# Feed-forward up projection from seven block products, and a down projection that reads its activations back from DRAM

## The chip, the cores and the metric

One core of a Trainium2 chip runs the whole program. The metric is the device time of one execution in microseconds (us). The kernel before was timed in three runs: median 1926.27 us, from 1924.97 to 1929.52. A matmul here has a weight of 128 x 128 and a moving operand of 128 x 512 or 128 x 256; float32 operands are split into a high and a low part (`hi`, `lo`), and a product takes three matmuls (hi·hi, hi·lo, lo·hi).

## The reference, cut to what matters

One decoder layer over 1024 tokens of width 1024. The change touches its last part only:

```
x = x + merged @ w_out
u = rmsnorm(x) * norm_ffn
h = causal_dwconv3(u @ w_up)          # w_up: 1024 x 5632, three taps along the tokens, plus a bias
g, val = split(h, 2)                  # 2816 = 22 tiles of 128 channels each
x = x + (silu(g) * val) @ w_down      # w_down: 2816 x 1024
out = rmsnorm(x) * norm_final
```

## The kernel before, in words

All data lie with channels on the 128 partitions and tokens along the columns. `x2` (L833) holds x as eight tiles j of 128 channels x 1024 tokens. `out_tile(j, h, w)` (L843) adds merged @ w_out for tile j and token half h, and adds the squares to `ss`. `rms_rows` (L170) turns `ss` into 1/RMS along the columns of a PSUM bank; it has two small parts on TensorE, four transposes each. `norm2(h)` (L857) then scales each of the eight tiles of half h on VectorE (DVE), casts the high part on ScalarE (ACT), and subtracts for the low part on VectorE or GpSimd (POOL), tile by tile (`scale_split`, L189).

The up projection has 44 column tiles, gate and value tile of one f tile in turn. `up(i)` (L884) loads one tile of weights (512 KB, `load_w`, L103: DMA, cast on ACT, subtraction on DVE), and for each token half runs 8 contraction tiles x 3 matmuls of 512 columns into one bank. The convolution is taken straight from that bank: one activation on ACT and two multiply-adds on DVE per half. The first halves of three column tiles run while the second half of the tokens is normalised (L912). `act_group` (L920) makes the activations of two f tiles, split, and keeps them in SBUF. The down projection follows two f tiles later: `down` (L935) takes 6 matmuls for an output tile and a token half, and adds the bank to `x2` on DVE. The last four f tiles are taken by tokens (512, 256, 256; L981), and each set of tokens is normalised and stored beside the next.

Every engine and the DMA queue of SyncE (SP) runs its instructions in order. What that order is, is fixed when the program is built: a planner (`schedule_with_timeline_sim`, L1078) takes, engine by engine, the earliest instruction of the program text whose inputs are there by its own estimate of time. `step` (L184) pins TensorE work behind a given instruction. Buffers come from pools with tags; a tile of the same tag waits until the last reader of the one before it is done. PSUM has seven working banks in this part (L831). The small tiles `sq` and `ut` share four buffers of tag `tmp`.

## Time and profile before

| what | value |
|---|---|
| median of three runs | 1926.27 us (1924.97 to 1929.52) |
| profiled execution | span 1923.5 us; the page gives it by its span alone |
| busy share of the span | TensorE 98%, VectorE 54%, ScalarE 39%, GpSimd 8% |
| mean granted TensorE clock | 0.995 of full speed |
| instructions on TensorE | 8916 matmuls |

The span is the time from the first to the last instruction of one profiled execution. A busy share is an average over stages with different limits; a stage has to be read by itself. The part that the change rewrites runs from 1183.67 us, the first matmul of the up projection, to the end of the span.

### The profile page before, as it was taken

The page shows a single profiled execution, that of the slowest core. Times are in us where ns is not written, and L with a number is a line of the kernel's source. Part 1 is how long each engine was busy: PE and PEld are TensorE (multiplying, and loading weights), DVE is VectorE, ACT ScalarE, POOL GpSimd, SP SyncE. Part 2 cuts the span into 40 slices and gives each one's busy share as a digit, 9 for nine tenths or more (in the row PEclk, how much of TensorE's full clock was granted, in tenths as well). Part 3 has the DMA queues.
Part 4 walks back from the last instruction along what each step waited for, and adds up shares of the span by engine and source line. Part 5 has one row for each costly group of instructions (what it writes and reads, how often), then busy time and mean ns, then how long its engine had stood idle before and what let it go on. Part 6 is the DMA issues. An engine that isn't in the chain of part 4 may idle for free.

```text
span 1923.5 us, 22457 instructions
## 1 busy us (share of the span) xinstructions
PE 1891.8 (98%) x8916; PEld 1555.9 (81%) x8916; DVE 1033.5 (54%) x1697; ACT 748.8 (39%) x1210; POOL 144.9 (8%) x122
## 2 busy tenths in 40 slices
PE   7999999999999999999999999999999999999997
PEld 6888888888878787877888887888888888888887
DVE  5742782751365554656664426654555455545546
ACT  5353682662355554546432313422222222222232
POOL 0100330420000000000040022000000000000002
PEclk9999999999999999999999999999999999999999
DMA  4230231433412223125453410111111111111112
GB/s 149 95 104 33 99 111 34 135 116 110 167 42 86 79 82 102 41 99 181 164 176 112 150 55 34 55 44 52 47 44 55 44 55 44 44 55 44 55 44 88
DMA packets 60235, 160.20 MB, mean 83 GB/s; under 512 B 6561, under 2 KB 13153, under 8 KB 59618
## 3 DMA queue, kind: packets, MB, share of 16 engines
q1 hardware_dynamic: 57392, 149.38, 22.5%
q0 software_dynamic: 1728, 8.39, 1.3%
q8 instruction: 70, 1.15, 0.2%
q10 hardware_dynamic: 1010, 1.00, 0.2%
q14 instruction: 35, 0.29, 0.0%
HBM read 127.71 MB, written 31.03 MB: 83 GB/s over the span
## 4 chain that ended last, share of the span: by engine, by line
PE 94%; DVE 2%; ACT 2%; DMA 1%; issue 1%; POOL 0%; SPq 0%; ACTq 0%; DVEq 0%; POOLq 0%
PE p_bank L119 42%; PE p_big L119 19%; PE p_half L119 16%; PE p_bank L261 2%; PE p_bank L260 2%; PE p_bank L259 2%; PE p_po L718 2%; PE p_sc L670 2%; PE p_pt L693 2%; PE p_sc L669 1%; PE p_bank L553 1%; PE p_bank L320 0%; DMA yps<-yp_d 0%; PE p_bank L807 0%; ACT mt L518 0%
## 5 line engine op out<-in xcount | busy, mean ns | idle before, releaser
L101 DVE TENSOR_TENSOR wlo<-wraw,whi 128x1024 fp32r<-128x1024 f32 x146 | 183.9, 1260 | 319.2 <-ACT whi L108 319.1
L108 ACT CAST whi<-wraw 128x1024 fp32r<-128x1024 f32 x146 | 153.3, 1050 | 438.2 <-PE p_bank L119 316.5
L119 PE MATMUL p_bank<-u2h,whi 128*128 128x512 f32 x704 | 274.7, 390 | 0.0
L119 PE MATMUL p_bank<-u2l,whi 128*128 128x512 f32 x704 | 274.6, 390 | 0.0
L119 PE MATMUL p_bank<-u2h,wlo 128*128 128x512 f32 x704 | 274.4, 390 | 0.0
L119 PE MATMUL p_bank<-act,whi 128*128 128x512 f32 (+1 forms) x720 | 210.9, 376 | 0.0
L899 DVE SCALAR_TENSOR_TENSOR ffn_tmp<-p_bank,vec,ffn_tmp 128x511 f32<-128x511 f32 (+1 forms) x176 | 131.3, 746 | 95.0 <-ACT ffn_tmp L897 93.5
L119 PE MATMUL p_big<-uh,whi 128*128 128x512 f32 (+1 forms) x416 | 157.6, 379 | 0.5 <-ACT whi L108 0.5
L119 PE MATMUL p_big<-uh,wlo 128*128 128x512 f32 (+1 forms) x416 | 157.5, 379 | 0.5 <-DVE wlo L101 0.5
L119 PE MATMUL p_big<-ul,whi 128*128 128x512 f32 (+1 forms) x416 | 157.0, 378 | 0.0
L119 PEld LDWEIGHTS p_bank<-u2h,wlo 128*128 128x128 f32 x704 | 132.5, 188 | 27.6
L119 PEld LDWEIGHTS p_bank<-u2l,whi 128*128 128x128 f32 x704 | 132.5, 188 | 27.5
L119 PEld LDWEIGHTS p_bank<-u2h,whi 128*128 128x128 f32 x704 | 132.5, 188 | 27.5
L119 PE MATMUL p_half<-uh,whi 128*128 128x512 f32 x384 | 153.5, 400 | 0.0
L119 PE MATMUL p_half<-ul,whi 128*128 128x512 f32 x384 | 153.2, 399 | 0.0
L119 PE MATMUL p_half<-uh,wlo 128*128 128x512 f32 x384 | 152.4, 397 | 0.0
L119 PEld LDWEIGHTS p_bank<-act,whi 128*128 128x128 f32 x720 | 132.2, 188 | 24.5
L944 DVE TENSOR_TENSOR x<-x,p_bank 128x512 f32<-128x512 f32 (+1 forms) x168 | 109.2, 659 | 52.8 <-PE p_bank L119 52.2
L119 PE MATMUL p_bank<-act,wlo 128*128 128x512 f32 (+1 forms) x360 | 135.4, 376 | 0.0
L168 POOL TENSOR_TENSOR ss<-ss,sq 128x512 f32<-128x512 f32 (+1 forms) x24 | 29.0, 1210 | 841.3 <-ACT sq L167 841.1
L897 ACT ACTIVATE ffn_tmp<-p_bank,vec 128x512 f32<-128x512 f32 x88 | 68.2, 775 | 58.7 <-PE p_bank L119 58.6
L119 PEld LDWEIGHTS p_big<-uh,wlo 128*128 128x128 f32 x416 | 79.1, 190 | 14.6 <-DVE wlo L101 0.8
(267 smaller groups left out, 3353.3 us busy)
## 6 DMA issues: line engine op xcount, KB each, us to landing
wraw<-in_w_in_dram SPq DMA_DIRECT2D x48, 512.0 KB, 3.3
wraw<-in_f_up_dram SPq DMA_DIRECT2D x44, 512.0 KB, 3.2
g_d<-gt SPq DMA_DIRECT2D x48, 256.0 KB, 2.0
gt<-g_d SPq DMA_DIRECT2D x48, 256.0 KB, 3.4
wraw<-in_f_down_dram SPq DMA_DIRECT2D x22, 512.0 KB, 3.2
mt<-acs_d SPq DMA_DIRECT2D x16, 512.0 KB, 4.1
xt<-in_x_dram SPq DMA_DIRECT2D x8, 512.0 KB, 7.5
wraw<-in_w_z_dram SPq DMA_DIRECT2D x8, 512.0 KB, 3.2
```

The costliest lines, as they stand in the source:

```text
L101: eng.tensor_tensor(lo, src, hi.bitcast(F32), op=ALU.subtract)
L108: nc.scalar.copy(hi, raw)
L119: m = nc.tensor.matmul(o, lhsT=wt, rhs=ah[part], start=first and i == 0, stop=last and i == 2)
L259: nc.tensor.matmul(ps, lhsT=a, rhs=hi[:, c], start=k == 0, stop=False)
L260: nc.tensor.matmul(ps, lhsT=a, rhs=lo[:, c], start=False, stop=False)
L261: nc.tensor.matmul(ps, lhsT=ul[t // 4][:, k, q], rhs=hi[:, c], start=False, stop=k == NT - 1)
L670: nc.tensor.matmul(pss[:, 0:w], lhsT=Q2[h][hp, qs], rhs=KL[hp, j0:j0 + w], start=False, stop=True)
L693: nc.tensor.transpose(pt[:, off + (i - qq[0]) * P:off + (i - qq[0] + 1) * P], in_=probs[i][:, kb * P:(kb + 1) * P], identity=ident)
L718: nc.tensor.matmul(po[:, q0:q0 + w], lhsT=VV[:, kb, h, :], rhs=t[:, o:o + w], start=pc == 0 and i == 0, stop=last and i == len(prods) - 1)
L897: nc.scalar.activation(a, ps, AF.Identity, bias=vec[:, V_FB + i:V_FB + i + 1], scale=w[2])
L899: nc.vector.scalar_tensor_tensor(out=a[:, s:], in0=ps[:, 0:512 - s], scalar=w[2 - s], in1=a[:, s:], op0=ALU.mult, op1=ALU.add)
L944: nc.vector.tensor_tensor(o, o, ps, op=ALU.add)
```

## The change

The up projection of one f tile is a product of 2 x 2 blocks: the weights of its gate tile (A11 and A12, contraction tiles 0 to 3 and 4 to 7) and of its value tile (A21, A22), times the normalised tokens (B11 and B21 for tokens 0 to 511, B12 and B22 for 512 to 1023). The change forms it from seven block products of 12 matmuls, with sums of blocks as operands. The sums of the weights, S1 to S4, are made for every f tile on GpSimd (`up_sums`). The sums of the tokens, T1 to T4, are made once, in `norm_second`. The seven weight blocks of an f tile are split into a ring of ten buffers, ten products ahead (`split_next`); six of them exist until the second normalisation is through. The products land in four banks (`pair`; `first_pair` for the first f tile, in another order), and VectorE and ScalarE add them up in one tile `cc` (`ca` gate, `cb` value, 1024 tokens each). `conv_act` convolves from `cc` and writes the activations to DRAM (`act_d`).

The down projection comes afterwards, in four passes: token half h, output tiles 0 to 3 or 4 to 7. A pass keeps four banks over all 22 f tiles. The activations of a half are read back, split (`act_group`), and kept for two passes; the down weights are loaded once per pass. x goes to DRAM (`x2_d`) as it is made and comes back as `xh0` and `xh1`, as the normalisation now overwrites `x2`. Only the last four f tiles of the last pass are taken by tokens (256, 256). The start of `load_w` and the old functions `up`, `act_group`, `down`, `last_down` are replaced; lines left out of the diff are `hl` (the two halves of a tile), the lists that name the blocks, `last_norm` and `last_down`, which do for one half what they did before.

```diff
+    def load_w(ap, own=None, after=None, raw=None):
+        raw = wpool.tile([P, 1024], F32, name="wraw", bufs=WRAW) if raw is None else raw
...
-    u2h = [slot(h, [P, NT, 512], R32, f"u2h{h}") for h in range(2)]
-    u2l = [slot(2 + h, [P, NT, 512], R32, f"u2l{h}") for h in range(2)]
+    x2_d = dpool.tile([2, P, NT, 512], F32, name="x2_d")
+    act_d = dpool.tile([FT, P, 1024], F32, name="act_d")
...
+    B11, B21, B22 = [hl(slot(i, HL, R32, n)) for i, n in enumerate(("b11", "b21", "b22"))]
...
+            nc.sync.dma_start(x2_d[h][:, j, :], o)
...
-        def norm2(h):
-            q = slice(h * 512, (h + 1) * 512)
-            rb, m = yield from rms_rows(sp, ss[:, q], 4)
+        u0, u1 = [[x2[k][:, h] for k in range(NT)] for h in (LO, HI)]
+        def norm_first():
+            rb, m = yield from rms_rows(sp, ss[:, LO], 4)
             for k in range(NT):
-                ut = sp.tile([P, 512], F32, name="ut", tag="tmp", bufs=4)
-                scale_split(u2h[h][:, k, :], u2l[h][:, k, :], x2[k][:, q], ut, vec[:, V_NF + k:V_NF + k + 1], rb,
+                hi, lo = (B11, B21)[k // 4]
+                scale_split(hi[:, k % 4, :], lo[:, k % 4, :], u0[k], u0[k], vec[:, V_NF + k:V_NF + k + 1], rb,
                             nc.gpsimd if k % 2 else nc.vector)
+            yield m
+        def norm_second(T1, T2, T3, T4):
+            rb, m = yield from rms_rows(sp, ss[:, HI], 4)
+            for k in (4, 5, 6, 7, 0, 1, 2, 3):
+                nc.vector.scalar_tensor_tensor(out=u1[k], in0=u1[k], scalar=vec[:, V_NF + k:V_NF + k + 1], in1=rb,
+                                               op0=ALU.mult, op1=ALU.mult)
+                if k >= 4:
+                    nc.scalar.copy(B22[0][:, k - 4, :], u1[k])
+                    sub_lo(nc.gpsimd, B22[1][:, k - 4, :], u1[k], B22[0][:, k - 4, :])
+                else:
+                    r1, r2, r3, r4 = [tmp("tr") for _ in range(4)]
+                    nc.vector.tensor_tensor(r1, u1[k], u0[k], op=ALU.subtract)
+                    nc.gpsimd.tensor_tensor(r3, u1[k + 4], u1[k], op=ALU.subtract)
+                    nc.vector.tensor_tensor(r2, u1[k + 4], r1, op=ALU.subtract)
+                    nc.gpsimd.tensor_tensor(r4, u0[k + 4], r2, op=ALU.subtract)
+                    for (hi, lo), r, eng in ((T1, r1, nc.vector), (T3, r3, nc.gpsimd), (T2, r2, nc.vector),
+                                             (T4, r4, nc.vector)):
+                        nc.scalar.copy(hi[:, k, :], r)
+                        sub_lo(eng, lo[:, k, :], r, hi[:, k, :])
...
+        T1, T2 = [hl(upool.tile(HL, R32, name=f"t{i + 1}", tag=f"uh{i}")) for i in range(2)]
+        T3, T4 = [hl(slot(4 + i, HL, R32, f"t{3 + i}")) for i in range(2)]
...
+        def up_sums(i, t):
+            a, b, s12, s34 = raw_blocks(t)
+            nc.sync.dma_start(a, f_up[2 * i])
+            nc.sync.dma_start(b, f_up[2 * i + 1])
+            g = nc.gpsimd
+            g.tensor_tensor(s12[:, LO], b[:, LO], b[:, HI], op=ALU.add)
+            g.tensor_tensor(s12[:, HI], s12[:, LO], a[:, LO], op=ALU.subtract)
+            g.tensor_tensor(s34[:, LO], a[:, LO], b[:, LO], op=ALU.subtract)
+            g.tensor_tensor(s34[:, HI], a[:, HI], s12[:, HI], op=ALU.subtract)
...
+        FIRST = ("A11", "A12", "S1", "S4", "S3", "S2", "A22")
+        ORDER = ("A11", "S2", "S3", "S1", "A12", "A22", "S4")
+        ring, parts = [], {}
+        todo = [(i, name) for i in range(FT) for name in (ORDER if i else FIRST)]
...
+        def split_next():
...
+            i, name = todo[n_split[0]]
+            hi, lo = ring[n_split[0] % len(ring)]
+            n_split[0] += 1
+            if i not in blocks:
+                blocks[i] = up_sums(i, raws)
+            nc.scalar.copy(hi, blocks[i][name])
+            sub_lo(nc.vector, lo, blocks[i][name], hi)
+            parts[i, name] = hi, lo
+        def prod(ps, i, name, b, first=True):
+            w = parts[i, name]
+            for k in range(4):
+                c = slice(k * P, (k + 1) * P)
+                m = mm3([ps], (w[0][:, c], w[1][:, c]), [(b[0][:, k, :], b[1][:, k, :])], first and k == 0, k == 3,
+                        skip_group_check=not first)
+            if len(ring) > 6:
+                split_next()
+            return m
+        def conv_act(i):
+            ca, cb, v, g = [cc[:, n, :] for n in range(4)]
+            for t, c, acc in ((2 * i + 1, cb, v), (2 * i, ca, g)):
+                w = [vec[:, V_FW + 3 * t + k:V_FW + 3 * t + k + 1] for k in range(3)]
+                nc.scalar.activation(acc, c, AF.Identity, bias=vec[:, V_FB + t:V_FB + t + 1], scale=w[2])
                 for s in (1, 2):
+                    nc.vector.scalar_tensor_tensor(out=acc[:, s:], in0=c[:, 0:1024 - s], scalar=w[2 - s],
+                                                   in1=acc[:, s:], op0=ALU.mult, op1=ALU.add)
+            nc.scalar.activation(g, g, AF.Silu)
+            nc.vector.tensor_tensor(g, g, v, op=ALU.mult)
+            nc.sync.dma_start(act_d[i], g)
+        def first_pair():
+            u2_, u3_ = tmp("U2"), tmp("U3")
+            b1 = bank()
+            m = prod(b1, 0, "A11", B11)
+            yield m
+            nc.scalar.copy(u2_, b1)
+            m = prod(b1, 0, "A12", B21, first=False)
+            yield m
+            nc.scalar.copy(ca[:, LO], b1)
+            b5 = bank()
+            prod(b5, 0, "S1", T1)
+            nc.scalar.copy(cb[:, HI], b5)
+            prod(b5, 0, "S4", B22, first=False)
+            b7 = bank()
+            prod(b7, 0, "S3", T3)
+            nc.vector.tensor_tensor(u3_, u2_, b7, op=ALU.add)
+            b6 = bank()
+            prod(b6, 0, "S2", T2)
+            nc.vector.tensor_tensor(u2_, u2_, b6, op=ALU.add)
+            nc.vector.tensor_tensor(u3_, u3_, b6, op=ALU.add)
+            nc.gpsimd.tensor_tensor(cb[:, HI], cb[:, HI], u3_, op=ALU.add)
+            nc.vector.tensor_tensor(ca[:, HI], u2_, b5, op=ALU.add)
+            m = prod(b7, 0, "A22", T4, first=False)
+            nc.vector.tensor_tensor(cb[:, LO], u2_, b7, op=ALU.add)
+            yield m
+        def pair(i):
+            u2_, u3_ = tmp("U2"), tmp("U3")
+            b1, b6 = bank(), bank()
+            prod(b1, i, "A11", B11)
+            prod(b6, i, "S2", T2)
+            nc.scalar.copy(u3_, b1)
+            nc.vector.tensor_tensor(u2_, u3_, b6, op=ALU.add)
+            b7 = bank()
+            prod(b7, i, "S3", T3)
+            nc.vector.tensor_tensor(u3_, u2_, b7, op=ALU.add)
+            b5 = bank()
+            prod(b5, i, "S1", T1)
+            nc.vector.tensor_tensor(cb[:, HI], u3_, b5, op=ALU.add)
+            prod(b1, i, "A12", B21, first=False)
+            nc.scalar.copy(ca[:, LO], b1)
+            prod(b7, i, "A22", T4, first=False)
+            nc.vector.tensor_tensor(cb[:, LO], u2_, b7, op=ALU.add)
+            prod(b5, i, "S4", B22, first=False)
+            nc.vector.tensor_tensor(ca[:, HI], u2_, b5, op=ALU.add)
+        blocks[0] = up_sums(0, slot(3, [P, 4, 1024], F32, "raw0"))
+        for _ in range(3):
+            hi, lo = [wpool.tile([P, 1024], R32, name=n, bufs=WHL) for n in ("whi", "wlo")]
+            ring += [(hi[:, c], lo[:, c]) for c in (LO, HI)]
+        for _ in range(6):
+            split_next()
+        n = norm_second(T1, T2, T3, T4)
+        g = first_pair()
+        m = step(m, g)
+        m = step(m, n)
+        m = step(m, g)
+        m = step(m, n)
+        more = upool.tile([P, 2, 4, 512], R32, name="ring", tag="ul0")
+        ring += [(more[:, 0, r, :], more[:, 1, r, :]) for r in range(4)]
+        raws = upool.tile([P, 4, 1024], F32, name="raws", tag="ul1")
+        split_next()
+        cc = slot(3, [P, 4, 1024], F32, "cc")
+        ca, cb = cc[:, 0, :], cc[:, 1, :]
+        for _ in range(5):
+            split_next()
+        run(g)
+        conv_act(0)
+        for i in range(1, FT):
+            pair(i)
+            conv_act(i)
+        stage = upool.tile([P, 4, 1024], F32, name="stage", tag="ul1")
...
+        def act_group(q, h, home):
+            t = home(HL, R32, f"act{h}_{q}")
...
+            for f in range(0, min(4, FT - 4 * q), 2):
+                raw = stage[:, n_act[0] % 2, :].rearrange("p (f t) -> p f t", f=2)
+                n_act[0] += 1
+                f0 = 4 * q + f
+                nc.sync.dma_start(raw, act_d[f0:f0 + 2].rearrange("f p t -> p f t")[:, :, h * 512:(h + 1) * 512])
+                fs = slice(f, f + 2)
+                nc.scalar.copy(hi[:, fs, :], raw)
+                sub_lo(nc.vector, lo[:, fs, :], raw, hi[:, fs, :])
...
+        def load_down(gr, part):
+            raw = stage[:, 2 + n_w[0] % 2, :]
+            n_w[0] += 1
+            return load_w(f_down[gr, part], raw=raw)
...
+        homes = [[in_slot(0), in_u("uh1"), in_slot(4), in_u("uh0"), in_slot(1), in_slot(5)],
+                 [in_slot(2), in_u("ul0"), in_slot(0), in_u("uh1"), in_slot(4), in_u("uh0")]]
...
+        def down_pass(h, part, acts, xh, grs):
+            bs = [bank() for _ in range(4)]
+            for gr in grs:
+                hi, lo = load_down(gr, part)
+                order = [(f, j) for f in range(2) for j in range(4)]
+                if gr == grs[-1]:
+                    order.sort(key=lambda x: x[1])
+                for f, j in order:
+                    c = slice(f * 512 + j * P, f * 512 + (j + 1) * P)
+                    m = mm3([bs[j]], (hi[:, c], lo[:, c]), [acts[2 * gr + f]], gr == grs[0] and f == 0,
+                            gr == grs[-1] and f == 1)
+                    if gr == grs[-1] and f == 1:
+                        o = xh[:, 4 * part + j, :]
+                        nc.vector.tensor_tensor(o, o, bs[j], op=ALU.add)
...
+        acts = [[], []]
+        for q in range(6):
+            acts[0] += act_group(q, 0, homes[0][q])
+        xh0 = load_x(0, in_slot(3))
+        down_pass(0, 0, acts[0], xh0, range(11))
+        squares(0, range(4), xh0)
+        for q in range(2):
+            acts[1] += act_group(q, 1, homes[1][q])
+        down_pass(0, 1, acts[0], xh0, range(11))
+        squares(0, range(4, 8), xh0)
+        for q in range(2, 6):
+            acts[1] += act_group(q, 1, homes[1][q])
+        xh1 = load_x(1, in_slot(1))
+        run(last_norm(0, xh0, slice(0, 512)))
+        down_pass(1, 0, acts[1], xh1, range(11))
+        squares(1, range(4), xh1)
+        down_pass(1, 1, acts[1], xh1, range(11 - NL))
+        wl = [load_down(gr, 1) for gr in range(11 - NL, 11)]
...
+        qs = (slice(0, 256), slice(256, 512))
+        *_, m = last_down(qs[0], range(4, 8))
+        n = last_norm(1, xh1, qs[0])
+        m = step(m, last_down(qs[1], (4,)))
+        m = step(m, n)
+        m = step(m, last_down(qs[1], (5, 6)))
+        m = step(m, n)
+        m = step(m, last_down(qs[1], (7,)))
         run(n)
+        run(last_norm(1, xh1, qs[1]))
```

## Rows read from the trace of the kernel before

**Rows 1.** The page, busy time by engine, and the granted TensorE clock in 40 slices.

```profile
PE 1891.8 (98%) x8916; PEld 1555.9 (81%) x8916; DVE 1033.5 (54%) x1697; ACT 748.8 (39%) x1210; POOL 144.9 (8%) x122
PEclk9999999999999999999999999999999999999999
```

**Rows 2.** The page, the chain that ended last, by engine.

```profile
PE 94%; DVE 2%; ACT 2%; DMA 1%; issue 1%; POOL 0%; SPq 0%; ACTq 0%; DVEq 0%; POOLq 0%
```

**Rows 3.** Busy time by stretch: length, engines, then granted clock, DMA share, GB/s.

```profile
1187.00:1190.00 3.00, 0.01 (x1) 0.04 (x1) 2.08 (x3) 1.56 (x2) 0.24 (x1) 0.93 0.01 4
1190.00:1193.00 3.00, 3.00 (x10) 2.53 (x10) 2.57 (x7) 0.20 (x1) 0.00 (x0) 0.50 0.24 74
1276.00:1864.00 588.00, 588.00 (x2592) 486.47 (x2591) 314.30 (x486) 146.28 (x162) 0.00 (x0) 1.00 0.14 49
```

**Rows 4.** Timeline of TensorE: start, us, operation; matmuls of 512 columns, up projection.

```profile
1219.81 0.39 PE L119 MATMUL p_bank<-u2l,whi 128*128 128x512 f32 x1
...
1234.09 0.39 PE L119 MATMUL p_bank<-u2l,whi 128*128 128x512 f32 x1
```

**Rows 5.** Timeline of TensorE, matmuls of 256 columns and the last ones.

```profile
1900.07 0.28 PE L119 MATMUL p_bank<-act,wlo 128*128 128x256 f32 x1
...
1903.31 0.28 PE L119 MATMUL p_bank<-act,wlo 128*128 128x256 f32 x1
...
1911.26 0.88 PE L119 MATMUL p_bank<-act,w_last 128*128 128x256 f32 x6
```

**Rows 6.** Timeline of TensorE, start of the up projection.

```profile
1183.67 0.39 PE L119 MATMUL p_bank<-u2h,whi 128*128 128x512 f32 x1
...
1189.99 1.08 PE L175 MATMUL p_st<-cst,ss 128*128 128x128 f32 x4 [3.43 <-DVE ss L168]
1190.73 0.78 PE L119 MATMUL p_bank<-u2h,whi 128*128 128x512 f32 x1
...
1197.36 0.60 PE L181 MATMUL p_st<-cst,rs_r 128*128 128x128 f32 x4
```

**Rows 7.** Waits of TensorE: total us, times, longest.

```profile
PE p_st L175 <- DVE ss L168: 5.4, 2, 3.4
```

**Rows 8.** Groups of VectorE: busy us, mean ns, idle before.

```profile
L101 DVE TENSOR_TENSOR act<-ffn_tmp,act 128x1024 fp32r<-128x1024 f32 x22 | 26.9, 1223 | 12.9 <-ACT act L931 12.9
L416 DVE SCALAR_TENSOR_TENSOR va<-vs,va 128x1024 f32<-128x1024 f32 x4 | 4.9, 1221 | 0.0
L944 DVE TENSOR_TENSOR x<-x,p_bank 128x512 f32<-128x512 f32 x152 | 102.9, 685 | 50.0 <-PE p_bank L119 49.6
L191 DVE SCALAR_TENSOR_TENSOR ut<-x,vec,p_st 128x512 f32<-128x512 f32 x16 | 11.1, 739 | 0.8 <-PE p_st L181 0.8
```

**Rows 9.** Timeline of VectorE: start, us, operation; subtractions of 512 columns.

```profile
1176.92 3.05 DVE L101 TENSOR_TENSOR u2l<-ut,u2h 128x512 fp32r<-128x512 f32 x2
...
1205.79 0.68 DVE L101 TENSOR_TENSOR u2l<-ut,u2h 128x512 fp32r<-128x512 f32 x1
...
1207.13 1.32 DVE L101 TENSOR_TENSOR u2l<-ut,u2h 128x512 fp32r<-128x512 f32 x1
```

**Rows 10.** Timeline of GpSimd: the same operation beside those of rows 9.

```profile
1176.42 3.01 POOL L101 TENSOR_TENSOR u2l<-ut,u2h 128x512 fp32r<-128x512 f32 x2 [0.90 <-ACT u2h L192]
...
1206.60 1.29 POOL L101 TENSOR_TENSOR u2l<-ut,u2h 128x512 fp32r<-128x512 f32 x1 [0.67 <-ACT u2h L192]
```

**Rows 11.** Groups of ScalarE: busy us, mean ns, idle before.

```profile
L928 ACT ACTIVATE ffn_tmp<-ffn_tmp 128x1024 f32<-128x1024 f32 x22 | 23.3, 1061 | 45.6 <-DVE ffn_tmp L907 45.6
L192 ACT CAST u2h<-ut 128x512 fp32r<-128x512 f32 x16 | 9.9, 621 | 10.1 <-DVE ut L191 9.8
```

**Rows 12.** DMA issues: size, median us to landing.

```profile
wraw<-in_f_up_dram SPq DMA_DIRECT2D x44, 512.0 KB, 3.2
g_d<-gt SPq DMA_DIRECT2D x48, 256.0 KB, 2.0
gt<-g_d SPq DMA_DIRECT2D x48, 256.0 KB, 3.4
```

More of the change, by code (lines that the diff above doesn't have):

```diff
@@ L118, in mm3 @@
             for o, ah in zip(outs, a):
-                m = nc.tensor.matmul(o, lhsT=wt, rhs=ah[part], start=first and i == 0, stop=last and i == 2)
+                m = nc.tensor.matmul(o, lhsT=wt, rhs=ah[part], start=first and i == 0, stop=last and i == 2,
+                                     **kw)
         return m.ins
```

145 lines of the change are left out of this document (51 added, 94 removed).

## The prediction

> **What bounds the kernel now.** First the page's busy time: TensorE is busy for 1891.8 of 1923.5 us, at a granted clock of nine tenths or more in every slice [rows 1]. Then the chain: TensorE carries 94% of it [rows 2]. Then busy time by stretch: in the 588 us from 1276 to 1864, up and down projection in turn, TensorE has no gap, VectorE is busy for 314 us and ScalarE for 146 [rows 3]. Last the timeline: 63 matmul intervals take 14.28 us, so one matmul of 512 columns costs 0.2267 us [rows 4]; 27 of 256 columns take 3.24 us, 0.120 us each [rows 5]. So this part is a queue of matmuls, and every matmul taken out is worth its interval as long as the other engines keep up. The one hole is at the start of the up projection: after 12 matmuls TensorE waits 3.43 us for the squares of the last output tile [rows 6, 7], and comes back at a granted clock of 0.50, the lower level (1.2 GHz), for the 3 us of the next stretch [rows 3].
>
> **TensorE's work, counted.** Before: up 44 tiles x 2 halves x 8 x 3 = 2112 matmuls of 512; down 18 f tiles x 8 x 2 x 3 = 864 plus 4 x 8 x 3 = 96 of 512, and 192 of 256. After: 22 x 7 x 12 = 1848 of 512 in the up projection; down 3 passes x 264 plus 18 x 4 x 3 = 1008 of 512, and 4 x 4 x 2 x 3 = 96 of 256. Removed: 216 x 0.2267 + 96 x 0.120 = 49.0 + 11.5 = 60.5 us. The rest of the sum is what TensorE has to wait for that it does not wait for now.
>
> **The second normalisation (the largest cost).** Before, the first halves of three column tiles, 72 matmuls or 16.3 us, cover it. After, only A11 x B11 and A12 x B21 are ready, 24 matmuls; the third product needs T1 of all four contraction tiles. Up to the squares nothing changes: again 12 matmuls, then the same wait. Then 12 matmuls from 1190.73 at the lower clock at first, to about 1194.0, four transposes of 0.60 [rows 6], so 1/RMS is there at 1194.6. From there VectorE has 8 scalings of 0.74 [rows 8] and, for each of four k, r1, r2 and the low parts of T1, T2, T4: 20 operations of 0.68 alone [rows 9]. That is 5.9 + 13.6 = 19.5 us. GpSimd has 16 operations of 1.29 us (four low parts of B22, r3, r4, the low part of T3), 20.6 us. Side by side they hinder each other: two subtractions on VectorE took 3.05 us while GpSimd did two of its own [rows 9, 10], against 1.36 alone, so a GpSimd operation costs VectorE 0.85. The scalings read a PSUM operand and I let them run beside GpSimd's first four; 12 x 0.85 = 10.2 goes on top: 29.7 us. ScalarE's 20 casts of 0.62, 12.4 us [rows 11], fit in. So the last T is there at 1224.3 and T1 some 3 us earlier, 1221. TensorE then still has 3 matmuls of S1 (9 trickled in before) and four products of 2.72 us, 11.6 us, and about 2 us at the lower clock: the first pair ends at 1235. Without the wait it would end at 1194.6 + 13.6 = 1208. Cost 27 us. Bounds: with no hindrance T1 comes after 16.5 us, cost 16; with all 16 GpSimd operations counted, and S4 kept back until its bank is copied into `cc`, whose slot waits for the split of A22 behind this normalisation, 34.
>
> One rule speaks against this step. The Trainium skill, SBUF — State Buffer, section Who interferes with whom, says that a VectorE instruction with two SBUF inputs and a GpSimd instruction that reads SBUF exclude each other for the whole instruction. The trace comes near it: the subtraction issued at 1207.13 took 1.32 us, and ended 0.56 us after GpSimd's, which had begun at 1206.60 [rows 9, 10]. By it the stage would take 13.6 + 20.6 = 34 us in place of 30.
>
> **A pair in the steady state.** TensorE: 84 x 0.2267 = 19.04 us. VectorE: 7 splits x 0.68, 5 additions from banks x 0.685, 4 multiply-adds and one product of 1024 columns x 1.22 [rows 8, 9] = 4.8 + 3.4 + 4.9 + 1.2 = 14.3 us, with four GpSimd sums x 0.85 on top 17.7. ScalarE: 7 casts and 2 copies x 0.62, 3 passes of 1024 x 1.06 [rows 11] = 8.8 us. GpSimd 4 x 1.29 = 5.2 us. All fit, VectorE at 93%. The order fits too, just: S4 and A22 add into banks that VectorE must read first. Between the end of S4 and the next A22 lie five products, 13.6 us; in them VectorE has one addition 0.7, the convolution 4.9, the product 1.2, three splits 2.0, two additions 1.4, and 3.4 for GpSimd: 13.6. The weights come in time: A11 of a block may be loaded three products before its split, 8.2 us, against 3.2 us to landing [rows 12] and 1.3 for the split of the block before; behind it on SyncE's queue stands only the write of an activation, which nobody needs for many us. The ring is ten products, 27 us, ahead. I take 3 us in all, for the first pairs behind the wait, when the ring is not full; bounds 0, and 20 if VectorE is late by 1 us in each of 21 pairs.
>
> **From up to down.** Slots come free product by product in the last pair, and the weight splits have ended ten products before, so VectorE can split the first activations (2.0 us to write, 3.4 to read back, 1.06 cast, 1.22 subtraction [rows 8, 11, 12]) under the last products: an f tile of early pairs is long in DRAM. I take 2 us. Bounds 0; and if the first down matmul stood behind the last convolution in VectorE's order, 0.7 + 4.9 + 1.2 and that round trip of 7.7, 14.
>
> **The passes.** A group of 24 matmuls takes 5.44 us; its weights cost 3.2 us of DMA, 1.06 ScalarE and 1.22 VectorE, so they stay hidden, although twice as many are loaded (44). x out and back, 16 writes and two reads, and the activations, lie beside TensorE's work: 0. The 128 additions into `x2` that fall away were hidden too: 0. The tail after the last matmul, from 1912.1 to 1923.5 [rows 5], is the same chain; the last steps have less cover (12 and 24 matmuls of 256 in place of 36 and 24), for which I take 1 us, bounds -1 and 3.
>
> **Sum.** -60.5 + 27 + 3 + 2 + 1 = -27.5 on a span of 1923.5: 1896.0. The median lies 2.8 us above the span; 1926.3 - 27.5 = 1899.
>
> **Rivals.** (1) The wait at the start is mostly hidden: VectorE and GpSimd don't meet and the T come after 16.5 us. -60.5 + 16 and nothing else gives 1882. For it: the planner may place GpSimd's sums beside the scalings. Against: both have about 20 us to do in the same 20 us.
>
> (2) VectorE becomes the bound of the pair: each GpSimd operation stops it for its whole 1.29 us [rows 10]. 14.3 + 5.2 = 19.5 against 19.04, 0.45 x 21 = 9 us, and 4 us more at the start: 1912. This is the rule above; the single subtraction speaks for it, the two in a row show 0.85.
>
> (3) Slower than before: the banks. If VectorE's fixed order puts two more splits (1.4 us) and the wait for the Silu (1.06) ahead of the two additions that A22 waits for, TensorE stands 2.4 us in each pair: 21 x 2.4 = 50 in place of 3, which gives 1946. It decides from (60.5 - 30)/21 = 1.45 us a pair. For it: the list above has no slack at all. Against: part of the convolution of the value half may start before S4 ends, and the planner takes what is ready.
>
> (4) It balances within 0.2%, which is about what a measurement of this kernel can tell from no change: (3) with 1.3 to 1.6 us a pair.
>
> **Chances.** Forecast, 1884 to 1910: 0.55. (1) 0.11, (2) up to 1922 0.15, (4) 0.04, (3) 0.15. Faster by over 0.2%: 0.81; within: 0.04; slower: 0.15. The range 1880 to 1924 leaves out the far end of (1) and most of (3) and (4).
>
> **What would show it.** 1848 and 1104 matmuls in the two parts; a hole of 20 us or more on TensorE in front of S1 x T1, released by a low part of T1 on VectorE, with a lower clock behind it; pairs 19.0 to 19.3 us apart; GpSimd busy some 5 to 6 us in each; no wait of TensorE for `whi`, `wlo` or act tiles over 3 us after the last pair. A regular wait in each pair for `cb` or U3 on VectorE would make the forecast wrong, to (2) or (3); a hole under 15 us to (1).

## The result, and the profile after

The changed kernel takes 1905.49 us (median of 4, from 1904.46 to 1907.18) against 1926.56 us of the kernel before on the same chip: ratio 0.9895, 95% interval 0.9881 to 0.9909, 21 us faster. Ratios here and below are estimated from the runs of both kernels in one experiment, and can differ from the quotient of the medians by 0.001. The forecast was 1899 in a range of 1880 to 1924. The profiled execution has a span of 1902.7 us, 20.8 less than before.

The page gives the busy time by engine, the clock in 40 slices, and the chain by engine [rows 1, 2]: TensorE has 312 matmuls less, GpSimd works twice as long, and one slice holds a clock of six tenths.

```profile
PE 1849.9 (97%) x8604; PEld 1505.3 (79%) x8604; DVE 1085.2 (57%) x1591; ACT 826.1 (43%) x1351; POOL 292.7 (15%) x220
...
PEclk9999999999999999999999999699999999999999
...
PE 81%; DVE 7%; DMA 4%; ACT 3%; issue 3%; POOL 1%; SPq 0%; ACTq 0%; DVEq 0%; POOLq 0%
```

The waits of TensorE from the up projection on [rows 7]. The first line is the second normalisation, the second the wait of the second f tile for its first sum, `U L1018` the wait of A22 x T4 for its bank.

```profile
PE p_bank L119 <- ACT t L897: 12.3, 6, 7.7
...
PE p_bank L119 <- ACT ring L954: 2.6, 1, 2.6
...
PE p_bank L119 <- DVE t L101: 2.1, 4, 1.4
...
PE p_bank L119 <- DVE U L1018: 1.5, 3, 0.9
```

TensorE's time line at the start [rows 6]: the squares end a wait of 2.39 us (3.43 before); then A12, the four transposes, and a hole of 7.72 us with single matmuls behind it. S4 x B22 begins at 1224.97, A22 x T4 ends at 1232.13, and behind A11 x B11 the second f tile waits 2.59 us for a split sum.

```profile
1188.22 0.63 PE L176 MATMUL p_st<-cst,ss 128*128 128x128 f32 x4 [2.39 <-DVE ss L169]
...
1199.75 0.79 PE L119 MATMUL p_bank<-t,whi 128*128 128x512 f32 x1 [7.72 <-ACT t L897]
...
1224.97 1.05 PE L119 MATMUL p_bank<-b,whi 128*128 128x512 f32 x2
...
1232.13 2.93 PE L119 MATMUL p_bank<-b,ring 128*128 128x512 f32 x12
1237.66 1.19 PE L119 MATMUL p_bank<-t,ring 128*128 128x512 f32 x4 [2.59 <-ACT ring L954]
```

The four transposes of 1188.22 and the twelve matmuls behind them take 3.21 us, up to the next transposes. In the kernel before they took 4.64 us, from 1189.99 to its matmul of 1194.63, at a granted clock of 0.50 in most of it [rows 3, 6]. That is chance, and no merit of the change: of the twelve kernels here that have the same work on TensorE up to there, the changed one among them, seven took 4.8 us in their profiled run and five 3.2 to 3.3. The lines are one of before, one of the changed kernel, and a stretch of one of the seven (the run without sums, below), with its granted clock of 0.64.

```profile
1194.63 0.39 PE L119 MATMUL p_bank<-u2h,whi 128*128 128x512 f32 x1
...
1191.43 0.60 PE L182 MATMUL p_st<-cst,rs_r 128*128 128x128 f32 x4
...
1186.90:1191.70 4.80, 4.80 (x17) 3.83 (x18) 1.70 (x7) 0.21 (x1) 0.00 (x0) 0.64 0.00 0
```

Busy time by stretch [rows 3]: the second normalisation, where TensorE's clock was granted at 0.59 on average, and the steady pairs, where it is busy for 258.57 of 260 us.

```profile
1192.00:1224.00 32.00, 17.60 (x36) 9.08 (x35) 28.91 (x28) 13.65 (x23) 23.53 (x16) 0.59 0.00 1
...
1340.00:1600.00 260.00, 258.57 (x1122) 209.28 (x1120) 186.71 (x228) 110.69 (x163) 73.41 (x52) 1.00 0.25 79
```

VectorE and GpSimd in that stage [rows 9, 10], in that order. Of VectorE's subtractions with two inputs in SBUF, those that begin while one of GpSimd's is under way take 1.00 to 1.76 us, and each ends about 0.55 us after it, as the single one before did (0.56 [rows 9, 10]). The one at 1210.50 is there first and takes 0.68; GpSimd's, which begins 0.22 us behind it, takes 1.59 in place of the 1.27 to 1.28 that it needs where it begins alone. The eight scalings run beside GpSimd's subtractions for 0.67 us each.

```profile
1192.06 5.36 DVE L884 SCALAR_TENSOR_TENSOR x<-x,vec,p_st 128x512 f32<-128x512 f32 x8 [1.04 <-PE p_st L182]
1197.34 1.71 DVE L891 TENSOR_TENSOR tr<-x 128x512 f32<-128x512 f32 x1
1199.08 1.65 DVE L893 TENSOR_TENSOR tr<-x,tr 128x512 f32<-128x512 f32 x1
...
1210.50 0.68 DVE L891 TENSOR_TENSOR tr<-x 128x512 f32<-128x512 f32 x1
...
1222.30 1.60 DVE L101 TENSOR_TENSOR t<-tr,t 128x512 fp32r<-128x512 f32 x1
```

```profile
1193.54 3.73 POOL L101 TENSOR_TENSOR b<-x,b 128x512 fp32r<-128x512 f32 x3 [9.03 <-ACT b L887]
1197.24 1.25 POOL L892 TENSOR_TENSOR tr<-x,x 128x512 f32<-128x512 f32 x1
1198.46 1.71 POOL L101 TENSOR_TENSOR b<-x,b 128x512 fp32r<-128x512 f32 x1
...
1210.72 1.59 POOL L892 TENSOR_TENSOR tr<-x,x 128x512 f32<-128x512 f32 x1 [0.69 <-DVE t L101]
```

The chain through one steady pair: start, us, what. It goes round: load of the raw weights, GpSimd's sums, cast and split, convolution, the splits behind it, and the next load 19.35 us later.

```profile
1464.40 4.49 DMA raws<-in_f_up_dram
...
1469.02 1.96 POOL raws L931
...
1471.04 1.16 issue
1472.20 1.30 POOL raws L932
1473.51 0.63 ACT ring L954
1474.17 1.24 DVE ring L101
...
1475.93 2.46 DVE cc L976 x2
...
1478.92 1.28 DVE cc L976
...
1483.75 4.68 DMA raws<-in_f_up_dram
```

What the chain gives as issue is a third sum, as GpSimd's time line has it: S1, S3 and S2 one after another.

```profile
1469.02 1.96 POOL L931 TENSOR_TENSOR raws<-raws 128x512 f32<-128x512 f32 x1 [13.52 <-DMA raws<-in_f_up_dram]
...
1470.95 1.28 POOL L933 TENSOR_TENSOR raws<-raws 128x512 f32<-128x512 f32 x1
...
1472.20 1.29 POOL L932 TENSOR_TENSOR raws<-raws 128x512 f32<-128x512 f32 x1
```

The splits, in groups over 17 pairs [rows 8]: 762 ns each, and VectorE idle for 77.7 us in front of them, 4.6 a pair.

```profile
L101 DVE TENSOR_TENSOR wlo<-raws,whi 128x512 fp32r<-128x512 f32 x70 | 52.7, 762 | 45.2 <-ACT whi L954 45.2
...
L101 DVE TENSOR_TENSOR ring<-raws,ring 128x512 fp32r<-128x512 f32 x48 | 36.2, 762 | 32.5 <-ACT ring L954 32.5
```

### The profile page after: what moved, and what is told of

It reads as the page before. It is cut to its first block, busy times and chain, and to the rows that moved or that the text cites. A ratio compares the mean times of both kernels' runs of the same rounds, so it can differ in the third digit from the quotient of the medians.

```text
span 1902.7 us, 22283 instructions
## 1 busy us (share of the span) xinstructions
PE 1849.9 (97%) x8604; PEld 1505.3 (79%) x8604; DVE 1085.2 (57%) x1591; ACT 826.1 (43%) x1351; POOL 292.7 (15%) x220
## 4 chain that ended last, share of the span: by engine, by line
PE 81%; DVE 7%; DMA 4%; ACT 3%; issue 3%; POOL 1%; SPq 0%; ACTq 0%; DVEq 0%; POOLq 0%
PE p_bank L119 31%; PE p_big L119 18%; PE p_half L119 16%; PE p_bank L261 2%; PE p_bank L260 2%; PE p_bank L262 2%; PE p_po L719 2%; DVE cc L976 2%; PE p_sc L671 2%; PE p_pt L694 2%; DMA raws<-in_f_up_dram 1%; DVE wlo L101 1%; PE p_sc L670 1%; PE p_bank L554 1%; POOL raws L931 1%
## 5 line engine op out<-in xcount | busy, mean ns | idle before, releaser
L101 DVE TENSOR_TENSOR wlo<-wraw,whi 128x1024 fp32r<-128x1024 f32 x81 | 102.6, 1267 | 159.2 <-ACT whi L108 159.1
L119 PE MATMUL p_bank<-t,whi 128*128 128x512 f32 x424 | 141.6, 413 | 14.7 <-ACT t L897 12.3
L108 ACT CAST whi<-wraw 128x1024 fp32r<-128x1024 f32 x81 | 84.9, 1048 | 134.9 <-PE p_big L119 68.4
L976 DVE SCALAR_TENSOR_TENSOR cc<-cc,vec 128x1023 f32<-128x1023 f32 x88 | 113.3, 1302 | 20.0 <-ACT cc L974 20.0
L119 PEld LDWEIGHTS p_bank<-t,whi 128*128 128x128 f32 x424 | 81.8, 195 | 41.9 <-ACT t L897 16.9
L119 PE MATMUL p_bank<-t,ring 128*128 128x512 f32 x420 | 100.8, 393 | 3.9 <-ACT ring L954 2.6
L119 PE MATMUL p_bank<-b,whi 128*128 128x512 f32 x328 | 102.9, 395 | 0.0
L101 DVE TENSOR_TENSOR wlo<-raws,whi 128x512 fp32r<-128x512 f32 x88 | 69.1, 795 | 49.1 <-ACT whi L954 49.1
L119 PEld LDWEIGHTS p_bank<-t,ring 128*128 128x128 f32 x420 | 78.4, 188 | 23.4 <-DVE U L1018 3.2
L119 PEld LDWEIGHTS p_big<-uh,whi 128*128 128x128 f32 x416 | 79.4, 191 | 14.9 <-ACT whi L108 1.6
```

The lines of the kernel that those rows point to most:

```text
L101: eng.tensor_tensor(lo, src, hi.bitcast(F32), op=ALU.subtract)
L108: nc.scalar.copy(hi, raw)
L119: m = nc.tensor.matmul(o, lhsT=wt, rhs=ah[part], start=first and i == 0, stop=last and i == 2, **kw)
L976: nc.vector.scalar_tensor_tensor(out=acc[:, s:], in0=c[:, 0:1024 - s], scalar=w[2 - s], in1=acc[:, s:], op0=ALU.mult, op1=ALU.add)
```

## The experiments

Where the up projection starts differs between profiled runs by up to 5 us, with identical code in front of it. So beside the medians stands the time within one trace, from the transposes of the squares (1188.22 in the changed kernel): to the end of the up projection (458.4 us), and to the end of the span (714.5). Some 1.6 us of such a time is chance: the 3.2 or 4.8 us that follow the squares.

### One part alone: eight products

The passes and the trip of the activations through DRAM stay, the seven products go; T1's buffer holds B12.

```diff
-        ORDER = ("A11", "S2", "S3", "S1", "A12", "A22", "S4")
+        FIRST = ORDER = ("A21", "A22", "A11", "A12")
+        def plain(i, half):
+            Bs, h = ((B11, B21), LO) if half == 0 else ((T1, B22), HI)
+            for c, names in ((cb, ("A21", "A22")), (ca, ("A11", "A12"))):
+                b1 = bank()
+                for n, name in enumerate(names):
+                    prod(b1, i, name, Bs[n], first=n == 0)
...
+                nc.scalar.copy(c[:, h], b1)
```

> One part of the change alone: the activations go to DRAM and the down projection runs in four passes as changed, but the up projection is formed from eight plain block products of 12 matmuls (no sums, four splits a pair, B12 and B22 in place of the T blocks). Theory A (the gain is the matmuls that fall away, the loss is the second normalisation; the trip through DRAM and the passes cost only the 2 us between up and down and 2 in the tail): TensorE's up projection takes 22 x 96 x 0.2267 = 478.8 us, the first pair has 36 matmuls that need no T, so that its wait nearly goes; from the first squares on 481 us in place of 458, so 1905.5 + 22.6 = 1928, the time of the kernel before within 3 us. Theory B (the passes and the trip win or lose more than 5 us that the counts don't show): under 1920 or over 1933.

1930.15 us, ratio to before 1.0022 (1.0011 to 1.0033): 3.7 us slower than before, 25 slower than the change. The up projection ends 480.8 us after the squares, against 481 expected, though the wait of the first pair doesn't go: TensorE waits for 1.49 and 4.46 us in the second normalisation, and no longer for the squares, as more products stand ahead of them. Between up and down it doesn't wait at all. From the last matmul to the end of the span it is 13.7 us, 11.4 before. So DRAM and the four passes bring nothing, and what they cost is the tail, some 2 us; most of the rest is the second normalisation. The whole gain is the products.

### The second normalisation: GpSimd's share on VectorE

```diff
-                    nc.gpsimd.tensor_tensor(r3, u1[k + 4], u1[k], op=ALU.subtract)
+                    nc.vector.tensor_tensor(r3, u1[k + 4], u1[k], op=ALU.subtract)
-                    nc.gpsimd.tensor_tensor(r4, u0[k + 4], r2, op=ALU.subtract)
+                    nc.vector.tensor_tensor(r4, u0[k + 4], r2, op=ALU.subtract)
-                    for (hi, lo), r, eng in ((T1, r1, nc.vector), (T3, r3, nc.gpsimd), (T2, r2, nc.vector),
+                    for (hi, lo), r, eng in ((T1, r1, nc.vector), (T3, r3, nc.vector), (T2, r2, nc.vector),
```

> In the second normalisation GpSimd's twelve operations on the T blocks (r3, r4 and the low part of T3, for four k) go to VectorE; its four low parts of B22 stay. Theory A (a GpSimd operation costs VectorE 0.85 us, its own operation takes 0.68): 12 x 0.68 = 8.2 us more and 10.2 us less, the first pair ends 2 us earlier, 1903.5. Theory B (they exclude each other for the whole 1.29 us): 12 x (1.29 - 0.68) = 7.3 us earlier, 1898. Theory C (no hindrance, VectorE alone is the bound of the stage): up to 8.2 us later, 1913.

1895.16 us, ratio 0.9840 (0.9826 to 0.9855): 10.3 us faster than the change. VectorE has twelve operations more and is done sooner: from the first scaling to the last part of T4 26.8 us in place of 35.0. The first pair ends 35.6 us after the squares in place of 43.9. In VectorE's time line the first subtraction still waits for GpSimd's last low part of B22 (1.70); from there they follow each other every 0.60 us, less than the 0.68 that each lasts.

```profile
1198.66 1.70 DVE L891 TENSOR_TENSOR tr<-x 128x512 f32<-128x512 f32 x1
1200.28 0.68 DVE L892 TENSOR_TENSOR tr<-x,x 128x512 f32<-128x512 f32 x1
1200.88 0.68 DVE L893 TENSOR_TENSOR tr<-x,tr 128x512 f32<-128x512 f32 x1
1201.49 1.28 DVE L101 TENSOR_TENSOR t<-tr,t 128x512 fp32r<-128x512 f32 x2
```

Theory A's 0.85 us falls, and theory B's 1898 is missed by 3 us on the other side: the first pair ends 8.3 us earlier, not 7.3, and the pairs behind it gain a little more. In the changed kernel one k took (1223.9 - 1197.34) / 4 = 6.6 us in the mean for five operations of VectorE and three of GpSimd; one after another they are 5 x 0.60 + 3 x 1.25 = 6.75. They take turns.

### The pairs: a bank of its own for A22

```diff
-            prod(b7, i, "A22", T4, first=False)
-            nc.vector.tensor_tensor(cb[:, LO], u2_, b7, op=ALU.add)
+            b4 = bank()
+            prod(b4, i, "A22", T4)
+            nc.vector.tensor_tensor(cb[:, LO], u3_, b4, op=ALU.add)
```

> A22 x T4 gets a bank of its own, so it no longer waits until VectorE has read the bank of S3 x T3 (the sum U3); nothing else is changed. Theory A (that wait is what a pair loses): in the 20 pairs after 1258 TensorE's A12 products run over by 3.1 us in sum, and the first matmul of A22 is about 0.1 us longer in a dozen of them, 1.2 us. Both go: the up projection is 4 us shorter, 1901.5 us. Theory B (the loop of the single buffer of raw weights, DMA, GpSimd's sums, splits, 19.4 us round, sets the pace): the pairs stay 19.3 to 19.4 us apart, the wait moves to the ring (whi, wlo), and the time stays at 1905.

1907.36 us, ratio 0.9900 (0.9885 to 0.9915): no gain. The wait for U3 is gone, and TensorE waits instead for the next reading of a bank (`cb`, L1021, before S4); the pairs stay 19.43 us apart (19.48 in the change). Theory A falls: the bank was where the delay showed, not what made it. Theory B had the time, but not the place: its wait for the ring does not appear.

### The pairs: no sums, and sums that nobody uses

```diff
+            if i == 0:
+                g.tensor_tensor(s12[:, LO], b[:, LO], b[:, HI], op=ALU.add)
...
+            else:
+                s12, s34 = b, a
```

> From the second f tile on, GpSimd's four sums of weight blocks are left out, and raw blocks stand in place of S1 to S4 (the sums of the weights are missing from what is computed). Theory A (TensorE loses its time to the bank that VectorE reads late, because the convolution stands ahead of it; GpSimd is not the cause): up projection 0 to 1.5 us shorter, plus the 2.6 us wait for the ring in the second pair, which had the sums in it: 1902 to 1905. Theory B (raw weights buffer and GpSimd set the pace): all of the waits go, 7 us or more, 1898. By the price of the prediction, 0.85 us of VectorE for each sum, VectorE would win 3.4 us a pair.

1894.68 us, ratio 0.9841 (0.9827 to 0.9856). The up projection is 7.2 us shorter; the pairs take 19.2 us each (19.22 to 19.24 from the fifth on), and the ring's wait of 2.6 us is gone. So the sums are the cause of what the pairs lose. The second kernel keeps them and cuts only the dependence:

```diff
+            if i:
+                s12, s34 = b, a
             return {"A11": a[:, LO], "A12": a[:, HI], "A22": b[:, HI], "S1": s12[:, LO], "S2": s12[:, HI],
```

> GpSimd makes all its sums of weight blocks as in the changed kernel, but from the second f tile on the splits take raw blocks, as in the run without sums (the sums of the weights are missing from what is computed). So GpSimd's load on SBUF stays and the chain DMA, sums, splits is cut. In the run without sums the up projection was 7 us shorter. Theory A (the chain: splits stand in VectorE's order, wait for the sums, and hold up the additions from banks behind them): most of the 7 us go here too, 1897 to 1899 us. Theory B (GpSimd keeps VectorE off SBUF, and that makes VectorE late): nothing goes, 1904 to 1905.

1922.60 us, ratio 0.9981 (0.9972 to 0.9990): both theories missed, it is 17 us slower than the change. From 1330 to 1600 TensorE waits for U3 nine times. GpSimd's sums, no longer in front of the splits, now run beside them and beside the convolution:

```profile
1481.64 1.29 POOL L932 TENSOR_TENSOR raws<-raws 128x512 f32<-128x512 f32 x1 [2.32 <-DMA raws<-in_f_up_dram]
1482.18 3.00 DVE L101 TENSOR_TENSOR ring<-raws,ring 128x512 fp32r<-128x512 f32 x2 [4.41 <-ACT ring L956]
...
1482.89 1.74 POOL L933 TENSOR_TENSOR raws<-raws 128x512 f32<-128x512 f32 x1
```

Two splits that take 1.28 alone take 3.00. In the change the chain had kept the two engines apart: VectorE stood idle while GpSimd summed. The run without sums differs from this one, in the program text, by GpSimd's operations alone, as both hold the raw blocks until the last split: beside VectorE's work, sums that nobody uses cost 28 us (1922.6 against 1894.7). What the chain alone costs, this run doesn't tell.

### The pairs: two ways to use the sums

On the run with VectorE's normalisation: ten half buffers for the raw weights, handed on one by one, so that loads start after the split of A11; or one buffer as before, with the sums on VectorE.

```diff
+                if i + 1 < FT and i + 1 not in halves and i in summed and (i, "A11") in parts:
+                    halves[i + 1] = {"A11": o["X"], "A12": o["Y"], "A21": o["A21"], "A22": o["A11"], "S1": o["S2"],
+                                     "S2": o["S3"], "S3": o["S1"], "S4": o["A12"], "X": o["A22"], "Y": o["S4"]}
...
+                if i + 1 in halves and i + 1 not in summed and all((i, n) in parts for n in ("S1", "S2", "S3", "A12")):
+                    sums(i + 1)
```

> On top of the run with VectorE's second normalisation (1895.2): the raw blocks of weights get ten half buffers in place of eight (the idle buffer wraw joins), and are handed on one by one, so that the next f tile's weights are loaded after the split of A11 and their sums are made after the split of A12, in place of loading after A12 and A22. The sums are used. Theory A (the chain of the raw buffer is what a pair loses): the up projection is 5 to 7 us shorter, 1889 us. Theory B (GpSimd's hold on SBUF is): 1895, as the sums are still made.

```diff
-            g = nc.gpsimd
+            g = nc.vector
             g.tensor_tensor(s12[:, LO], b[:, LO], b[:, HI], op=ALU.add)
```

> The run with VectorE's second normalisation (1895.2), with the sums of the weight blocks on VectorE too; one buffer of raw weights as before. GpSimd then does next to nothing in the up projection. Theory A (a GpSimd operation on SBUF shuts VectorE out for its whole 1.25 to 1.29 us and keeps the splits waiting longer; on VectorE the same sum takes 0.60): 4 x 0.60 = 2.4 us a pair on VectorE that has 4 us to spare, the pairs go from 19.4 to 19.2 us and the 2 to 3 us of waits in the second and third pair shrink: 1889 us. Theory B (the loop of the raw buffer, whoever makes the sums): pairs stay at 19.4, 1894. Theory C (VectorE becomes the bound, or its sums, which wait for a DMA, hold up the additions behind them): 1900 or more.

1897.14 us, ratio 0.9840 (0.9823 to 0.9856), and 1894.93, 0.9832 (0.9816 to 0.9848), against 0.9840 of the kernel they build on. In the steady pairs both reach what theory A wanted: 19.23 us, and TensorE without a gap. Busy time from 1340 to 1600, the ten halves and then the sums on VectorE:

```profile
1340.00:1600.00 260.00, 260.00 (x1137) 213.23 (x1137) 216.01 (x230) 116.60 (x161) 102.33 (x54) 1.00 0.24 81
```

```profile
1340.00:1600.00 260.00, 260.00 (x1137) 213.20 (x1137) 210.04 (x281) 111.81 (x159) 0.00 (x0) 1.00 0.24 81
```

With the sums on VectorE, 51 operations more, it is busy for 6 us less than beside GpSimd. The medians don't show the gain. The halves give it back in the third pair, in one wait of 4.9 us for U3: nine operations of GpSimd in a row slow VectorE down before it. With the sums on VectorE there is one wait of 3.0 us in the second pair; the kernel that it builds on also waits for 3.0 us in its second and third pair, in three parts. From the squares to the end of the up projection it is 451.2 and 446.3 us, against 449.2; the first two have the 4.8 us behind the squares, the last the 3.2. So in its trace the up projection with the sums on VectorE is 3 to 4 us shorter; why the time of the runs (1890.14 to 1896.91) doesn't tell it is open.

### Work for the hole

On the ten half buffers: banks of their own for S4 x B22 and A22 x T4 in the first pair, and two products of the second f tile under the normalisation; then the same with the sums on VectorE.

```diff
+            early.append(bank())
+            prod(early[0], 1, "A11", B11)
+            nc.scalar.copy(ss[:, LO], early[0])
+            m = prod(early[0], 1, "A12", B21, first=False)
...
+            b3, b5, b7, b6, b4 = [bank() for _ in range(5)]
+            prod(b3, 0, "S4", B22)
...
+            m = prod(b4, 0, "A22", T4)
```

> On top of the ten half buffers: in the first pair S4 x B22 and A22 x T4 get banks of their own, S4 runs first, and A11 and A12 of the second f tile are multiplied under the normalisation too (36 matmuls, 8.2 us, that TensorE did behind it). Theory A (TensorE stands idle for some 14 us of that stage beside VectorE, so this work is free): 4 us from the first pair's end and 5.4 from the second f tile, less 2 to 3 us in which the second f tile's S2 is waited for: 1881 to 1884 us. Theory B (VectorE, which has three more splits in the stage, sets the time until the ring is full again): the gain comes back as waits for the ring in the second and third pair, 1888 or more.

> The run with the stage filled and ten half buffers (1889.9), with the sums of the weights on VectorE. Theory A: the 6.9 us wait for the first split sum of the second f tile shrinks to 4 to 5 us (two sums at 0.60 in place of 1.3 to 1.7), the pairs behind it, which ran 19.7, 21.8, 16.2 us in turn, go to 19.2: 1884 us. Theory B: VectorE bound in the first pairs, no change, 1890.

1889.94 us, ratio 0.9809 (0.9794 to 0.9823), and 1888.49, 0.9803 (0.9786 to 0.9819). The work fits: in the stage TensorE is busy for 23.39 of 26.90 us and its clock is granted in full.

```profile
1194.70:1221.60 26.90, 23.39 (x82) 14.02 (x81) 26.77 (x43) 13.73 (x24) 5.10 (x4) 1.00 0.02 3
```

But the second f tile then waits 6.9 us for its first sum, not 2 to 3, and with the sums on VectorE 7.1: theory A was wrong there in both runs, and the times are those of theory B, though the wait is another; it is not the price of the sums. The raw buffer lies where x was, so in the second of the two runs its load is issued when the last T is made (1220.7) and lands at 1224.9. The last of the fill kernels loads the value weights before, into the idle `wraw`, and begins that pair with what they give:

```diff
+        wraw2 = wpool.tile([P, 1024], F32, name="wraw", bufs=WRAW)
+        nc.sync.dma_start(wraw2, f_up[3])
...
+        nc.vector.tensor_tensor(ss[:, HI], wraw2[:, LO], wraw2[:, HI], op=ALU.add)
...
+                prod(b5, 1, "S1", T1)
+                prod(b4, 1, "A22", T4)
```

> On top of the last of the runs with everything together (1887.4): the value weights of the second f tile are loaded into wraw before the normalisation, so that its S1 is there at the end of it, and S1 x T1 and A22 x T4 of the second f tile come first in that pair (24 matmuls, 5.4 us); its gate weights are loaded a second time behind it, for S2 to S4. Theory A (the 6.7 us wait for the second f tile's first sum is the time of a load, two sums and a split, and TensorE can work in it): 4 to 5.4 us less, 1882 to 1883. Theory B (VectorE is behind by that time in any case, and the wait comes back in front of S2): 1886 to 1888.

1880.25 us, ratio 0.9764 (0.9749 to 0.9779), with the tail below: 46 us less than before, 25 less than the change. The wait of 6.7 us is 0.6. The gain over 1887.4 is 7.1 us, more than the 4 to 5.4 of theory A: before, the matmuls behind that wait ran at the lower clock (0.53 granted over 4.6 us), and now at full clock. What is left shows in the same time line: S4 x B22, now early, waits for GpSimd's low part of B22.

```profile
1207.07 0.69 PE L119 MATMUL p_bank<-b,whi 128*128 128x512 f32 x1 [3.80 <-POOL b L101]
...
1228.80 1.25 PE L119 MATMUL p_bank<-t,ring 128*128 128x512 f32 x4 [0.61 <-ACT ring L959]
```

### The tail

```diff
-        NL = 2
+        NL = 3
```

> The last six f tiles of the last pass are taken by tokens, in place of four (NL = 3). Theory A (the tail is 2.0 us longer than before because the eight scalings of the first 256 tokens, 3.2 us on VectorE, stand ahead of the last addition): TensorE gets 2.9 us more cover behind them, the tail goes from 13.4 back to 11.4 us, at 24 x (2 x 0.120 - 0.2267) = 0.3 us of TensorE: 1903.8. Theory B (the scalings run where they are for want of something else): the tail stays at 13.4, 1905.8.

1904.49 us, ratio 0.9893 (0.9876 to 0.9909): no gain clear of noise. The wait for the last squares is 3.02 us in place of 3.73, but the scalings still stand ahead of the last addition: both parts of the first norm are pinned behind output tiles, and moved along. So, on the run with the stage filled and the sums on VectorE, the second part goes one tile forward as well:

```diff
-        m = step(m, last_down(qs[1], (5, 6)))
+        m = step(m, last_down(qs[1], (5,)))
         m = step(m, n)
-        m = step(m, last_down(qs[1], (7,)))
+        m = step(m, last_down(qs[1], (6, 7)))
```

> As the run before in this list, and in the tail the last six f tiles by tokens (NL = 3) with the second part of the first norm one output tile earlier, so that two tiles (4.3 us of TensorE) lie behind it in place of one (1.4 us). The run with NL = 3 alone kept the eight scalings (3.2 us) ahead of the last addition, as both parts had moved along. Theory A (the cover was what was missing): the last wait for the squares goes from 3.7 to about 1.7 us, less 0.3 for the narrower matmuls and up to 0.7 of wait in front of the second part: 1 us faster. Theory B: no change.

1887.39 us, ratio 0.9796 (0.9782 to 0.9811), against 1888.49; the medians alone don't tell. The trace does: the scalings (1869.78) now lie before the last two additions, the wait for the last squares is 1.84 us in place of 3.73, and from the last matmul to the end of the span it is 11.3 us in place of 13.4, or 13.7 in the run without it.

```profile
1869.78 3.22 DVE L1171 SCALAR_TENSOR_TENSOR x2h<-x2h,vec,p_st 128x256 f32<-128x256 f32 x8
...
1873.67 0.42 DVE L1208 TENSOR_TENSOR x2h<-x2h,p_bank 128x256 f32<-128x256 f32 x1 [0.34 <-PE p_bank L119]
1875.47 0.41 PE L176 MATMUL p_st<-cst,ss 128*128 128x128 f32 x2 [1.84 <-DVE ss L169]
```

## Why the prediction was right, step by step

| step of the prediction | forecast, us | measured, us |
|---|---|---|
| TensorE's work | -60.5 | 312 matmuls less on the page; 25 us lost again with eight products |
| The second normalisation | +27 | +26.5 |
| A pair in the steady state | +3 | +12.6 |
| From up to down | +2 | +1.9 |
| Tail | +1 | +2.0 |
| Wait for the squares, start of the part | 0 | -1.0, -0.7 |
| The clock behind the squares | 0 | -1.4 |
| Sum | -27.5 | -20.8 |

By the measured terms the sum is -60.5 + 26.5 + 12.6 + 1.9 + 2.0 - 1.7 - 1.4 = -20.6; 0.2 us is left over. The term of the clock (4.64 - 3.21) is chance, as shown above, and so is the -0.7.

**What bounds the kernel now** held. TensorE is the queue on both sides; every gain among these runs is matmuls taken out, or waits of TensorE made shorter, those in the tail included, with the clock that hung on them.

**The second normalisation.** The forecast had the last T at 1224.3 and the end of the first pair at 1235. The last part of T2 came at 1223.9 and the end of the pair at 1232.1; the last part of T4 came at 1227.1, under S4 x B22, so that TensorE didn't wait for it. The cost is 1232.1 less 1192.0 + 13.6, 26.5 us. But the parts of the term were wrong, and that they met is luck: the stage from 1/RMS (1192.0, not 1194.6) to 1223.9 took 2.1 us more than the 29.7 forecast, and what TensorE had left behind it 8.2 us in place of 10.7. S1, S3 and S2 had by then been multiplied one tile after another, as the T came, where the forecast had counted on nine matmuls of S1. For the same reason the sign named beforehand, a hole of 20 us or more in front of S1 x T1, didn't come: the longest wait is 7.72 us, ended by a cast of ScalarE, and the waits of the stage make 14.4 us in all. Read by its own words, the sign would have pointed to rival (1), at a cost of 26.5 us: what the stage costs is not the length of its first hole.

The price of GpSimd was wrong as well. A GpSimd operation that is there first stops a VectorE subtraction until it ends; "a GpSimd operation costs VectorE 0.85" came from two subtractions in a row that took 3.05 us [rows 9, 10]. But GpSimd's first had begun 0.50 us ahead of them: taking turns, with 0.75 of it left, gives 0.75 + 0.60 + 1.25 + 0.60 = 3.2. The rows had shown it, read so. The Trainium skill, SBUF — State Buffer, section Who interferes with whom, states the exclusion, and that a VectorE instruction with at most one SBUF input, outside the 2-port modes, is free of it; this trace agrees with both, by the subtractions of up to 1.76 us and the scalings of 0.67. So rival (2) had the mechanism and the forecast the better sum. The stage of 34 us that the rule gave in the prediction was too long as well, as it added single durations, 0.68 and 1.29. With the steps at which operations follow each other it is 5.4 + 20 x 0.60 + 12 x 1.25 = 32.4, against 31.8.

**A pair in the steady state** is the term that was mis-sized: 3 us forecast, 12.6 measured, within its bounds of 0 and 20. From 1232.13 to 1646.58 less nine matmuls of the down projection it is 412.4 us, against 21 x 19.04 = 399.8. It comes apart into
- 2.6 us, the wait of the second f tile for its first sum, the "first pairs behind the wait" that the forecast's 3 us were for;
- 1.6, matmuls at the lower clock behind it (twelve in 4.34 us in place of 2.72);
- 4.0: a pair without any wait takes 19.23 us, not 19.04 (three runs without a gap show it), so 0.19 x 21. In the run with the sums on VectorE, A11, S2 and A12 take the 2.72 us of 12 x 0.2267 [rows 4], and S3, S1, A22 and S4 2.76 to 2.77, spread over the product. The change of bank alone doesn't make it, as S2 begins in a new bank too; the length of 12 alone doesn't either, as the eight products ran at 0.2267 throughout. What does is open;
- about 4, the loop of the raw buffer: 16 pairs at 19.48 us on average, 0.25 more than without it. The forecast held that the weights come in time, A11 being "loaded three products before its split", and took GpSimd's sums as load on VectorE alone. In truth three sums, 4.5 us, stand between the landing of the weights and the split of S2, in a loop that must close in 19.2. Either cure closes it: more buffers, or sums at 0.6 on VectorE.

These make 12.2; 0.4 is left over. The list of VectorE's work ahead of A22, full with 13.6 us, was not what counted: A22's own bank won nothing. Nor did the sums cost VectorE 3.4 us a pair: its splits are 762 ns in place of 684, 0.5 a pair, because it idles while they run.

**From up to down** and **the passes**: 1.46 us for the first split weights and some tenths, as forecast. In the run with eight products the passes cost nothing but the tail, some 2 us.

**Tail**: the bounds were -1 to 3. VectorE's eight scalings stood ahead of the last addition, as "less cover" meant; the run with everything together shows it by removing it.

**Signs.** 1848 and 1104 matmuls, 5.5 us of GpSimd a pair and no wait over 3 us behind the last pair came as said; the pairs, 19.48 us apart, lie outside the 19.0 to 19.3 that were named.

**Rivals.** (1), 1882, needed VectorE and GpSimd not to meet; they did. (3), 1946, needed 2.4 us a pair at the banks; the whole loss in the pairs is 0.6. A time like that of (1) can be had in another way: with the hole filled, the sums off GpSimd, the second f tile's weights loaded early and the tail changed, 1880.

## What to carry to other kernels

Before an elementwise operation goes to GpSimd beside VectorE, ask whether both read two SBUF tiles: then the two take turns, and GpSimd's operation takes 1.25 us where VectorE itself needs 0.60. A product scheme with fewer matmuls moves work in front of the first product; look for products whose operands are there already, and load what the next tile needs before the stage and not behind it. Where a wait moves when its buffer is doubled, follow the chain once round: here it closed over a load four steps away.

## What the hardware showed that was not expected

- Subtractions on VectorE that last 0.68 us follow each other every 0.60, so a sum of single durations is 13% too long.
- The convolution's multiply-adds, which read two SBUF tiles, are longer beside GpSimd too: 1.67 us on average with GpSimd busy for 102 of 260 us (the ten halves), 1.28 with GpSimd idle (the sums on VectorE).

```profile
L1002 DVE SCALAR_TENSOR_TENSOR cc<-cc,vec 128x1022 f32<-128x1022 f32 (+1 forms) x53 | 87.4, 1668 | 9.3 <-ACT cc L1000 9.3
...
L976 DVE SCALAR_TENSOR_TENSOR cc<-cc,vec 128x1023 f32<-128x1023 f32 (+1 forms) x52 | 65.5, 1279 | 7.5 <-ACT cc L974 7.1
```

- In the second normalisation TensorE was granted 0.59 of its clock when it got single matmuls between waits, and S4 x B22 behind them took 4.40 us in place of 2.72. With 82 matmul records in the stage in place of 36, the granted clock was 1.00.
